# Four pairs in the third pass of w_down, casts of a pair gated by its buffers, two loads in buffers of v, and a longer lag for rows of q and k

## The chip, the cores and the metric

One Trainium2 chip, one of its cores. The metric is the device time of one execution in microseconds (us), the median of the runs. A core has engines that work in parallel, each through its own instructions in a fixed order: TensorE (PE, matmuls), VectorE (DVE), ScalarE (ACT), GpSimd (POOL), and SyncE (SP), which here only starts DMA transfers. An instruction that waits holds up everything behind it on its engine. Matmuls add up in PSUM, in eight banks; all else lies in SBUF.

## The reference

One encoder layer, x of 256 rows by 2048, all in float32:

```python
xn = rms_norm(h, norm1_g)
proj = xn @ w_in                      # 2048 x 5120: q, k, v, ga, gg
q, k = rope(rms_norm(q)), rope(rms_norm(k))
att = rms_norm(diff_attention(q, k, v, lam), subln_g) * (1 - lambda_init)
u = silu(layer_norm(causal_depthwise_conv(ga * sigmoid(gg))))   # 31 taps
h = h + concat([att, u]) @ w_out      # 2048 x 2048
hn = rms_norm(h, norm2_g)
a, bu = hn @ w_gate, hn @ w_up        # 2048 x 5632 each
y = h + (silu(a) * bu) @ w_down       # 5632 x 2048
```

## The kernel before

**Matmuls.** Every operand is split into a rounded part and a residue (`hi` and `lo`), and a product is three matmuls: hi by hi, lo by hi, hi by lo. The weights come as *chunks*, in the order in which they are multiplied. A plain chunk is 128 x 1024 values: SyncE loads it into a `raw` buffer (four of them, `RAW_BUFS`), ScalarE casts `whi` (L342), VectorE subtracts to get `wlo` (L351). For some, marked `by_dma`, ScalarE writes the negated raw into `wlo` (L345) and GpSimd starts a transfer that adds the weights to it (L346). There are four `whi` and four `wlo` buffers.

**Pairs.** In the feed-forward part (FFN) a block of the output is 256 x 1024, from two weight sides of 512 columns: 512 of w_gate and of w_up, or two neighbouring 512s of w_down. Most k-tiles (128 rows of the weights) go in by twos, one unit for each side: 12 matmuls, `multiply_two` (L1112, L1117). Written "g"/"u", or "G"/"U" where the `lo` is made by DMA. Others go in as a *pair* "s": two k-tiles and both sides in seven products by a fast scheme (as Strassen's), 21 matmuls in `multiply_pair` (L1090, L1091, L1092) for the 24 of a g and a u. A pair's weights must be prepared: SyncE loads `wb` (1 MB, L1051, two buffers), VectorE makes sums of them in `wt` (L1057 to L1059, one buffer), ScalarE casts three of its seven parts from `wb` (L1064) and four from `wt` (L1068) into `wh`, VectorE makes the residues `wl` of the three (L1072) and of the four (L1073). `wh` and `wl` have two buffers each. The other operand of a pair has forms of its own too, made by `pair_forms` (VectorE L971 to L976 and L980, ScalarE L965 to L968 and L978).

**The FFN.** Eleven blocks j of w_gate and w_up (j = 0 without pairs), and in three passes (`FGROUPS` = 4, 4 and 3 blocks j) the rows of w_down that those blocks feed; a pass has two blocks of output. `DOWN` has for each pass the k-tiles (j, t) that are pairs, and the order of units in its two blocks. At the end of a block the eight banks are added up: ScalarE copies the first product (L1095), VectorE adds five (`bank_sums`, L1194 to L1199, the first four of which free the banks that the next block's products take), then the g/u units' banks (L1213 in a block of w_gate and w_up, with the multiplication L1215 behind it; L1247 in one of w_down). After a block of w_gate and w_up its activation is transposed by TensorE (L918) into `ps_a` and copied by ScalarE: for a pair by `pair_forms`, else by L953, and for the very last block j = 10 through a copy `ac` (L951) first; VectorE makes its residue (L955).

**The order.** The program is written unit by unit in `run_chunks`; the engines then run in that order. Ahead of unit t's matmuls, a lookahead issues the preparation of later units: residues (`part`), casts from `wb` (`raw`), sums, casts with `lo` by DMA (`dma`), casts (`round`), loads. Each list goes on in order of units, up to some units ahead, and stops at the first that it may not issue. Chains of work beside it (`transposed`, attention) are generators, resumed a step at a time between units; if a unit's operand isn't written yet when its turn comes, they are resumed until it is. `LAG[0]` is the number of such steps by which the rows of q and k (normalisation and rotation, VectorE L704 to L707) are put off. In the same stretch VectorE also does the taps of the convolution (L592).

Of the kernel before, what the change touches and what calls it, by code (L numbers as in the profile page):

```python
# [13 lines left out]
F32 = mybir.dt.float32  # L14
# [5 lines left out]
P = 128  # L20
D = 2048
S = 256
NM = S // P
# [9 lines left out]
N = 512  # L33
# [16 lines left out]
NK = 2  # L50
# [11 lines left out]
RAW_BUFS = 4  # L62
# [1 line left out]

MINUS_FROM = 8

LAG = (3, 2, 6)
HL_BUFS = 4

KTILE_US = 1.30  # L70
# [19 lines left out]

DOWN = (dict(pairs=((1, 0), (1, 1), (2, 0)), order=("sgGsgGgsuUuUu",) * 2),
        dict(pairs=((4, 0), (4, 1), (5, 0)), order=("sgGsgGgsuUuUu",) * 2),
        dict(pairs=((8, 0), (8, 1), (9, 0)), order=("sGsGgsUUu", "sGsGGsUUu")))

RAW_AHEAD = 5
LOAD_AHEAD, DMA_AHEAD, SUMS_AHEAD, HI_AHEAD, LO_AHEAD = 9, 5, 5, 4, 3
# [18 lines left out]
def tile_block(  # L115
# [13 lines left out]
    pre = prestack.enter_context(tc.tile_pool(name="pre", bufs=2))  # L129
# [124 lines left out]
    def resume():  # L254
        for g in list(running):
            if next(g, StopIteration) is StopIteration:
                running.remove(g)
# [36 lines left out]
    chunks = []  # L294
    before = {}

    def block(w, cols, ks, xs, done=None, bkey=None, first=True, last=True, spare=False, cuts=()):

        ks = list(ks)
        cols = [(cols, N)] if isinstance(cols, int) else cols  # L300
        width = sum(n for _, n in cols)
        bkey = bkey if bkey is not None else ("b", len(chunks))
        i = 0
        cuts = list(cuts)
        while i < len(ks):
# [10 lines left out]
    def weights(parts):  # L316

        n = sum(w for _, _, _, w in parts)
        src = wts[next_weight[0] : next_weight[0] + P * n].rearrange("(p n) -> p n", n=n)
        placed_at.append((next_weight[0], n, parts))  # L320
        next_weight[0] += P * n
        return src

    def load_chunk(c):
        view = lambda t: t.rearrange("p (k n) -> p k n", n=c["width"])[:, : c["nk"]]
        c["view"] = view
        if c.get("spare_raw"):
            c["raw"] = view(early.tile([P, 4 * N], F32, tag="wb", name="raw")[:, : NK * N])
        else:
            c["raw"] = view(wp.tile([P, NK * N], F32, tag="raw", name="raw", bufs=RAW_BUFS))  # L330
        ks = c["ks"] if "ks" in c else range(c["k0"], c["k0"] + c["nk"])
        c["src"] = src = weights([(c["w"], k, col, n) for k in ks for col, n in c["cols"]])
        sp.dma_start(out=c["raw"].rearrange("p k n -> p (k n)"), in_=src)
# [75 lines left out]
    loaded, rounded, parted = [0], set(), set()  # L409
    pair_at, two_at = [], []  # L410

    def earlier(at, i, n):

        k = bisect.bisect_left(at, i) - n
        return at[k] if k >= 0 else None
# [38 lines left out]
    def may_round_raw(t, i):  # L454
        c = chunks[i]
        if "sides" not in c:
            return True
        o = earlier(pair_at, i, 2)
        return loaded[0] > i and o is not None and o < t
# [8 lines left out]
    def part_of(i):  # L468
        if i not in parted:
            parted.add(i)  # L470
            round_of(i)
            chunks[i]["split"](chunks[i])

    def run_chunks():
        n = len(chunks)
        pair_at.extend(i for i, c in enumerate(chunks) if "sides" in c)
        two_at.extend(i for i, c in enumerate(chunks) if "kind" in c and "sides" not in c)
        at = dict(part=0, dma=0, sums=0, round=0, minus=0, raw=0)
        first = next(i for i, c in enumerate(chunks) if "kind" in c)

        def until(what, do, stop, only=lambda c: True, may=lambda i: True):
            while at[what] < min(n, stop) and may(at[what]):
                if only(chunks[at[what]]):
                    do(at[what])
                at[what] += 1

        for t in range(n):
            if t >= first - AHEAD:
                until("part", part_of, t + 1 + LO_AHEAD)
                until("raw", lambda i: round_raw(chunks[i]), t + 1 + RAW_AHEAD, lambda c: "sides" in c,  # L490
                      lambda i: i <= t or may_round_raw(t, i))
                until("sums", sums_of, t + 1 + (SUMS_AHEAD if t >= first else 0), may=may_sum)
                until("dma", round_of, t + 1 + DMA_AHEAD, lambda c: c["by_dma"])
                until("round", round_of, t + 1 + (HI_AHEAD if t >= first else LO_AHEAD))
                load_until(t + 1 + LOAD_AHEAD)
            else:
                if t < len(XPARTS):
                    until("part", part_of, t + 2)
                else:
                    until("part", part_of, t + 1 + AHEAD)  # L500
                    until("minus", minus_of, min(t + 1 + MINUS_AHEAD, first), lambda c: c.get("minus"))
                    until("round", round_of, min(t + 1 + ROUND_AHEAD, first))
            part_of(t)
            chunks[t]["multiply"](chunks[t])
            if chunks[t].get("prompt") and chunks[t]["done"]:
                resume()
        while running:
            resume()
# [175 lines left out]
    def qk_rows(key, b, m, ps):  # L684
# [8 lines left out]
        pool.tensor_scalar(f, f, rstd1[m], 0.0, ALU.mult, ALU.add)  # L693
        yield from lag(LAG[0])
        qn = pre.tile([P, G, DH], F32, tag="va", name="qn")
        for j in range(G):
            act.activation(qn[:, j, :], ps[:, j * DH : (j + 1) * DH], AF.Copy, scale=f[:, j : j + 1])
        yield from lag(LAG[1])
        t1 = pre.tile([P, G, DH], F32, tag="vb", name="t1")
# [7 lines left out]
        dve.tensor_tensor(t1, t1, t2, ALU.add)  # L707
        yield from lag(LAG[2])
        yield from room(1)
# [351 lines left out]
    def round_raw(c):  # L1061
        if "hi" not in c:
            c["hi"] = ffn["pool"].tile([P, 7, N], F32R, tag="wh", name="wh", bufs=2)
            act.copy(c["hi"][:, 4:], c["b"][:, 1:])  # L1064
# [206 lines left out]
    for ks, first, last in ((range(0, 4), True, False), (range(4, 6), False, False), (range(6, 8), False, False),  # L1271
                            (range(8, 16), False, True)):
        for n in range(3):
            block("w_out", n * N, ks, fm, (lambda ps, n=n: out_done(n, ps)) if last else None,
                  bkey=("o", n), first=first, last=last, spare=n == 2)
    block("w_out", 3 * N, range(16), fm, lambda ps: out_done(3, ps))
    for i, c in enumerate(chunks[len(XPARTS) : -12]):
        c["spare_raw"] = i % 3 == 2
        c["minus"] = i >= MINUS_FROM and i % 6 == 4
# [59 lines left out]
```

## Time and profile before

| | |
|---|---|
| median of 3 runs | 1037.3 us (1037.26 to 1037.98) |
| the profiled execution | 1037.66 us, its span 1035.9 us |
| TensorE busy | 1028.0 us, 99% of the span |
| VectorE, ScalarE, GpSimd busy | 83%, 66%, 15% |
| memory read and written | 248.80 MB and 8.39 MB |
| granted TensorE clock, mean | 1.00 |

The span is the time from the first to the last instruction of the profiled execution; times inside the trace count from its start. A row of a timeline has start, duration, engine, line, operation, output and inputs, and in brackets the idle time before it and what ended it, where that is long enough to be named. Durations of TensorE overlap: the start of the next instruction tells its pace.

### The profile page before, as it was taken

The numbers are of one execution on the slowest core, as the hardware profiler recorded it, in microseconds if no ns is written. First come the engines' busy times: TensorE is split into PE (matmuls) and PEld (weight loads), VectorE is DVE, ScalarE is ACT, GpSimd is POOL, SyncE is SP. The second block draws the span as 40 slices with busy tenths as digits, with TensorE's granted clock in tenths as the row PEclk, the third lists the DMA queues.
The fourth block names the chain that finished last, engine by engine and source line by source line (L and its number), as shares of the span: only waits on it lengthen the run. The fifth ranks groups of instructions, "written<-read, shape, count | busy, mean of one in ns | idle before, by whom it ended". The sixth has DMA issues, their size and how long they took to land.

```text
span 1035.9 us, 13050 instructions
## 1 busy us (share of the span) xinstructions
PE 1028.0 (99%) x4641; PEld 849.0 (82%) x4641; DVE 862.7 (83%) x1087; ACT 685.8 (66%) x865; POOL 155.1 (15%) x198
## 2 busy tenths in 40 slices
PE   9999999999999999999999999999999999999998
PEld 7888888888888888788888888888888888888886
DVE  6699889897646699999978779999896697998983
ACT  6855567767756577777566667776765666767761
POOL 0040232411100101011011111110101121111121
PEclk9999999999999999999999999999999999999999
DMA  9967775676566669798889998987969999889896
GB/s 341 326 201 239 236 208 187 189 218 183 154 211 224 229 238 262 247 319 240 254 255 292 260 308 263 307 237 241 309 186 286 290 283 327 234 250 299 238 263 130
DMA packets 66065, 258.05 MB, mean 249 GB/s; under 512 B 7376, under 2 KB 8912, under 8 KB 58576
## 3 DMA queue, kind: packets, MB, share of 16 engines
q1 hardware_dynamic: 48944, 201.34, 53.7%
q0 software_dynamic: 16768, 55.58, 28.2%
q8 instruction: 36, 0.59, 0.2%
q10 hardware_dynamic: 288, 0.29, 0.1%
q14 instruction: 29, 0.24, 0.1%
HBM read 248.80 MB, written 8.39 MB: 248 GB/s over the span
## 4 chain that ended last, share of the span: by engine, by line
PE 83%; DVE 9%; DMA 3%; POOL 2%; ACT 1%; issue 1%; DVEq 0%; ACTq 0%
PE q L1112 23%; PE q L1117 12%; PE q L1090 9%; PE q L1091 9%; PE q L1092 9%; PE acc L387 6%; PE acc L381 6%; PE acc L382 6%; DVE y L592 5%; DVE wlo L351 3%; DMA raw<-in_wts_dram 3%; PE ps_a L918 1%; POOL rsq L220 1%; PE ps_s L727 1%; PE ps_o L805 1%
## 5 line engine op out<-in xcount | busy, mean ns | idle before, releaser
L342 ACT CAST whi<-raw 128x1024 fp32r<-128x1024 f32 (+1 forms) x262 | 270.5, 1042 | 102.8 <-PE acc L382 44.4
L351 DVE TENSOR_TENSOR wlo<-raw,whi 128x1024 fp32r<-128x1024 f32 (+1 forms) x174 | 209.1, 1210 | 71.4 <-ACT whi L342 68.4
L381 PE MATMUL acc<-whi,lhi 128*128 128x512 f32 x416 | 164.2, 395 | 1.2 <-ACT whi L342 1.2
L382 PE MATMUL acc<-whi,llo 128*128 128x512 f32 x416 | 162.2, 390 | 0.0
L1073 DVE TENSOR_TENSOR wl<-wt,wh 128x2048 fp32r<-128x2048 f32 x58 | 132.7, 2287 | 20.2 <-ACT wh L1068 20.1
L1064 ACT CAST wh<-wb 128x1536 fp32r<-128x1536 f32 x58 | 86.0, 1484 | 86.9 <-PE q L1091 54.0
L346 POOL DMA_DIRECT2D wlo<-in_wts_dram x74 | 65.1, 891 | 509.7 <-ACT wlo L345 486.0
L1068 ACT CAST wh<-wt 128x2048 fp32r<-128x2048 f32 x58 | 110.5, 1904 | 18.5 <-DVE wt L1059 18.4
L1090 PE MATMUL q<-wh,fhi 128*128 128x512 f32 x280 | 109.1, 390 | 0.4 <-DVE sum L1197 0.4
L1092 PE MATMUL q<-wl,fhi 128*128 128x512 f32 x280 | 109.0, 389 | 0.0
L1091 PE MATMUL q<-wh,flo 128*128 128x512 f32 x280 | 108.9, 389 | 0.0
L1072 DVE TENSOR_TENSOR wl<-wb,wh 128x1536 fp32r<-128x1536 f32 x58 | 101.6, 1751 | 2.1 <-ACT wh L1064 2.1
L592 DVE SCALAR_TENSOR_TENSOR y<-upad,cw,y 128x256 f32<-128x256 f32 x240 | 100.5, 481 | 3.2 <-ACT y L585 3.2
L387 PE MATMUL acc<-wlo,lhi 128*128 128x512 f32 x368 | 100.7, 395 | 0.5 <-DVE wlo L351 0.5
L381 PEld LDWEIGHTS acc<-whi,lhi 128*128 128x128 f32 x416 | 78.1, 188 | 18.4 <-ACT whi L342 2.3
L382 PEld LDWEIGHTS acc<-whi,llo 128*128 128x128 f32 x416 | 78.2, 188 | 16.0
L1117 PE MATMUL q<-wlo,chi 128*128 128x512 f32 x320 | 86.9, 393 | 0.0
L1112 PE MATMUL q<-whi,chi 128*128 128x512 f32 x320 | 85.8, 390 | 0.0
L1112 PE MATMUL q<-whi,clo 128*128 128x512 f32 x320 | 85.6, 389 | 0.0
L387 PEld LDWEIGHTS acc<-wlo,lhi 128*128 128x128 f32 x368 | 68.4, 188 | 14.6 <-DVE wlo L351 0.9
L345 ACT ACTIVATE wlo<-raw 128x1024 fp32r<-128x1024 f32 x74 | 78.2, 1056 | 0.0
L1057 DVE TENSOR_TENSOR wt<-wb 128x1024 f32<-128x1024 f32 x58 | 70.8, 1220 | 2.0 <-DMA wb<-in_wts_dram 1.6
(224 smaller groups left out, 1682.0 us busy)
## 6 DMA issues: line engine op xcount, KB each, us to landing
raw<-in_wts_dram SPq DMA_DIRECT2D x258, 512.0 KB, 5.6
wb<-in_wts_dram SPq DMA_DIRECT2D x57, 1024.0 KB, 7.9
wlo<-in_wts_dram POOLq DMA_DIRECT2D x74, 512.0 KB, 9.3
lod<-in_wts_dram POOLq DMA_DIRECT2D x14, 512.0 KB, 6.4
out_dram<-sum POOLq DMA_DIRECT2D x22, 256.0 KB, 7.2
h<-in_x_dram SPq DMA_DIRECT2D x4, 512.0 KB, 9.1
out_dram<-h POOLq DMA_DIRECT2D x8, 256.0 KB, 3.7
xt<-in_xt_dram SPq DMA_DIRECT2D x6, 256.0 KB, 6.8
```

The source lines that it names most:

```text
L342: act.copy(c["hi"], c["raw"])
L351: dve.tensor_tensor(c["lo"], c["raw"], c["hi"].bitcast(F32), ALU.subtract)
L381: pe.matmul(ps[m], xhi[:, ms], hi[:, j, :], start=c["first"] and j == 0, stop=False)
L382: pe.matmul(ps[m], xlo[:, ms], hi[:, j, :], start=False, stop=False)
L387: pe.matmul(ps[m], xhi[:, ms], lo[:, j, :], start=False, stop=c["last"] and j == nk - 1)
L592: dve.scalar_tensor_tensor(y[:, ct, :], src, wk, y[:, ct, :], ALU.mult, ALU.add)
L1073: dve.tensor_tensor(c["lo"][:, :4], c["t"], c["hi"][:, :4].bitcast(F32), ALU.subtract)
L1090: pe.matmul(ps, fhi[:, f, p, :], c["hi"][:, w], start=bool(first), stop=False)
L1091: pe.matmul(ps, flo[:, f, p, :], c["hi"][:, w], start=False, stop=False)
L1092: pe.matmul(ps, fhi[:, f, p, :], c["lo"][:, w], start=False, stop=bool(last))
L1112: pe.matmul(ps, plain[i][e][:, ms], hi[:, i, :], stop=False, start=i == e == 0 and bool(c["first"].get(qs[m])))
L1117: pe.matmul(sum_bank(c, qs[m]), plain[i][0][:, ms], lo[:, i, :], start=False, stop=i == 1 and bool(c["last"].get(qs[m])))
```

## The change

Lines of the kernel after are 2 to 9 further down than those of before: L351 is then L353, L951 L958, L953 L960, L1064 L1071, L1068 L1075, L1057 to L1059 L1064 to L1066, L1072 and L1073 L1079 and L1080, L1213 L1220, L1215 L1222.

```diff
-LAG = (3, 2, 6)
+LAG = (5, 2, 6)
...
-        dict(pairs=((8, 0), (8, 1), (9, 0)), order=("sGsGgsUUu", "sGsGGsUUu")))
+        dict(pairs=((8, 0), (8, 1), (9, 0), (10, 0)), order=("sGsgsUsu", "sGsgssUu")))
...
         if c.get("spare_raw"):
             c["raw"] = view(early.tile([P, 4 * N], F32, tag="wb", name="raw")[:, : NK * N])
+        elif "raw_tag" in c:
+            c["raw"] = view(pre.tile([P, NK * N], F32, tag=c["raw_tag"], name="raw", bufs=1))
...
         for t in range(n):
             if t >= first - AHEAD:
-                until("part", part_of, t + 1 + LO_AHEAD)
-                until("raw", lambda i: round_raw(chunks[i]), t + 1 + RAW_AHEAD, lambda c: "sides" in c,
+                until("part", part_of, t + 1 + LO_AHEAD, plain)
+                until("pair_part", part_of, t + 1 + LO_AHEAD, pair,
+                      lambda i: i <= t or plain(chunks[i]) or i in rounded)
+                until("raw", lambda i: round_raw(chunks[i]), t + 1 + RAW_AHEAD, pair,
                       lambda i: i <= t or may_round_raw(t, i))
                 until("sums", sums_of, t + 1 + (SUMS_AHEAD if t >= first else 0), may=may_sum)
                 until("dma", round_of, t + 1 + DMA_AHEAD, lambda c: c["by_dma"])
-                until("round", round_of, t + 1 + (HI_AHEAD if t >= first else LO_AHEAD))
+                ahead = HI_AHEAD if t >= first else LO_AHEAD
+                until("round", round_of, t + 1 + ahead, plain)
+                until("pair_round", round_of, t + 1 + ahead, pair, lambda i: i <= t or may_round_raw(t, i))
                 load_until(t + 1 + LOAD_AHEAD)
...
+    for m in range(NM):
+        chunks[RAW_BUFS + m]["raw_tag"] = f"v{m}"
```

In the third pass (10, 0) becomes a fourth pair: 6 matmuls fewer in two blocks. The casts and residues of a pair leave the common lists: a pair's casts are issued ahead of its turn only once it is loaded and the pair two back has been multiplied (`may_round_raw`), its residues only once it is cast. Chunks 4 and 5 (the first of full width) load into the buffers that v takes later, not into `raw` buffers that chunks 0 and 1 used: the wait of their loads for VectorE's L351 is gone, and each of the others that follow uses a `raw` buffer that came free earlier.

Outside of these first loads and of the rows of q and k, the order of instructions differs in two places: the first block with pairs (j = 1) and the end, from the last block j = 10 on. First j = 1, ScalarE's row before (`wh_3687` is the first pair's, `wh_3817` the second's; a name's number differs between the two kernels):

```order
L342 CAST whi_3753<-raw_3727 128x1024 [waits DMAHW0_49,DVE_49,PE_49]
L345 ACTIVATE wlo_3755<-raw_3727 128x1024 [waits PE_49]
L1068 CAST wh_3687<-wt_3600 128x2048
L907 CAST lhi_90<-ps_a_3773 128x512 [waits PE_49]
L907 CAST lhi_90<-ps_a_3778 128x512 [waits PE_49]
L342 CAST whi_3812<-raw_3731 128x1024 [waits DMAHW2_49,DVE_49,PE_49]
L345 ACTIVATE wlo_3814<-raw_3731 128x1024 [waits PE_49]
L1064 CAST wh_3817<-wb_3729 128x1536 [waits DMAHW1_49,DVE_49]
L1068 CAST wh_3817<-wt_3788 128x2048 [waits DVE_49]
```

and after:

```order
L344 CAST whi_3753<-raw_3727 128x1024 [waits DMAHW0_49,DVE_49,PE_49]
L347 ACTIVATE wlo_3755<-raw_3727 128x1024 [waits PE_49]
L914 CAST lhi_90<-ps_a_3772 128x512 [waits PE_49]
L914 CAST lhi_90<-ps_a_3777 128x512 [waits PE_49]
L344 CAST whi_3800<-raw_3731 128x1024 [waits DMAHW2_49,DVE_49,PE_49]
L347 ACTIVATE wlo_3802<-raw_3731 128x1024 [waits PE_49]
L1075 CAST wh_3687<-wt_3600 128x2048
L344 CAST whi_3841<-raw_3839 128x1024 [waits DMAHW4_49,DVE_49,PE_49]
L347 ACTIVATE wlo_3843<-raw_3839 128x1024 [waits PE_49]
L1071 CAST wh_3883<-wb_3729 128x1536 [waits DMAHW1_49]
L1075 CAST wh_3883<-wt_3833 128x2048 [waits DVE_49]
```

The first pair's L1068 has moved behind the next two casts. Two units later L342 and L345 of `raw_3897`, which is loaded behind the fourth pair's `wb`, stand ahead of the third pair's L1068 (of `wh_3889`).

The end, ScalarE before (`ac_8354` and `ac_8398` are the two halves of block 10's activation, `wh_8415` the first pair of the last block):

```order
L345 ACTIVATE wlo_8335<-raw_8214 128x1024 [waits DMASW4_49]
L1068 CAST wh_8331<-wt_8293 128x2048 [waits DVE_49]
L951 COPY ac_8354<-ps_a_8349 128x512 [waits PE_49,Activation_49]
L953 CAST lhi_90<-ac_8354 128x512 [waits Activation_49]
L342 CAST whi_8364<-raw_8247 128x1024 [waits DMAHW6_49]
L345 ACTIVATE wlo_8366<-raw_8247 128x1024 [waits DMASW0_49,PE_49]
L951 COPY ac_8398<-ps_a_8393 128x512 [waits PE_49]
L953 CAST lhi_90<-ac_8398 128x512 [waits Activation_49]
L1064 CAST wh_8415<-wb_8299 128x1536 [waits DMAHW0_49]
```

and after (`wh_8327` is pair (9,0) of the third pass's first block, `wh_8391` pair (10,0), `ac_8402` the half (10,1), which the g that comes next on TensorE reads as `ahi_3466`):

```order
L1071 CAST wh_8327<-wb_8210 128x1536 [waits DMAHW3_49,PE_49,Activation_49]
L1075 CAST wh_8327<-wt_8266 128x2048 [waits DVE_49]
L972 COPY af_8343<-ps_a_8338 128x512 [waits DVE_49,PE_49]
L974 CAST lhi_90<-af_8343 128x2x128 [waits Activation_49]
L975 ACTIVATE lhi_90<-af_8343 128x128
L985 CAST lhi_90<-fs_8368 128x4x128 [waits DVE_49]
L1071 CAST wh_8391<-wb_8272 128x1536 [waits DMAHW5_49,PE_49]
L344 CAST whi_8393<-raw_8274 128x1024 [waits DMAHW6_49]
L1075 CAST wh_8391<-wt_8354 128x2048
L958 COPY ac_8402<-ps_a_8397 128x512 [waits DVE_49,PE_49]
L960 CAST ahi_3466<-ac_8402 128x512 [waits Activation_49]
```

The casts of pair (10,0) now stand ahead of the copy and cast of (10,1). VectorE before, from the residues of pair (8,1):

```order
L1072 TENSOR_TENSOR wl_8272<-wb_8137,wh_8239 128x1536 [waits PE_49,Activation_49]
L1073 TENSOR_TENSOR wl_8272<-wt_8208,wh_8239 128x2048 [waits Activation_49]
L1213 TENSOR_TENSOR sum1_8257<-q6_7994,sum1_8257 128x512 [waits DVE_49,PE_49]
L1213 TENSOR_TENSOR sum3_8259<-q7_8173,sum3_8259 128x512 [waits PE_49]
L1215 TENSOR_TENSOR sum1_8257<-sum1_8257,sum0_8219 128x512 [waits DVE_49,Activation_49]
L1215 TENSOR_TENSOR sum3_8259<-sum3_8259,sum2_8258 128x512 [waits DVE_49,Activation_49]
L1057 TENSOR_TENSOR wt_8293<-wb_8212 128x1024 [waits DMAHW4_49]
L1058 TENSOR_TENSOR wt_8293<-wb_8212,wt_8293 128x512 [waits DVE_49]
L1059 TENSOR_TENSOR wt_8293<-wt_8293,wb_8212 128x512 [waits DVE_49]
```

and after:

```order
L1079 TENSOR_TENSOR wl_8263<-wb_8137,wh_8237 128x1536 [waits PE_49,Activation_49]
L1080 TENSOR_TENSOR wl_8263<-wt_8206,wh_8237 128x2048 [waits Activation_49]
L1064 TENSOR_TENSOR wt_8266<-wb_8210 128x1024 [waits DMAHW3_49,DVE_49]
L1065 TENSOR_TENSOR wt_8266<-wb_8210,wt_8266 128x512 [waits DVE_49]
L1066 TENSOR_TENSOR wt_8266<-wt_8266,wb_8210 128x512 [waits DVE_49]
L1220 TENSOR_TENSOR sum1_8248<-q6_7994,sum1_8248 128x512 [waits PE_49]
L1220 TENSOR_TENSOR sum3_8250<-q7_8171,sum3_8250 128x512 [waits PE_49]
L1222 TENSOR_TENSOR sum1_8248<-sum1_8248,sum0_8217 128x512 [waits DVE_49,Activation_49]
L1222 TENSOR_TENSOR sum3_8250<-sum3_8250,sum2_8249 128x512 [waits DVE_49,Activation_49]
L353 TENSOR_TENSOR wlo_8292<-raw_8139,whi_8270 128x1024 [waits DMASW6_49,DMASW3_49,DMAHW2_49,DMASW0_49,Activation_49]
L1079 TENSOR_TENSOR wl_8351<-wb_8210,wh_8327 128x1536 [waits PE_49,Activation_49]
L1080 TENSOR_TENSOR wl_8351<-wt_8266,wh_8327 128x2048 [waits Activation_49]
```

The sums of the next pair have moved ahead of L1213 and L1215, and the sums of (10,0) come two residues later. In all TensorE has 6 matmuls fewer, VectorE 17 instructions more, ScalarE 3, GpSimd 5 and SyncE 2 fewer.

More of the change, by code (lines that the diff above doesn't have):

```diff
@@ L477, in run_chunks @@
         two_at.extend(i for i, c in enumerate(chunks) if "kind" in c and "sides" not in c)
-        at = dict(part=0, dma=0, sums=0, round=0, minus=0, raw=0)
+        at = dict(part=0, dma=0, sums=0, round=0, minus=0, raw=0, pair_part=0, pair_round=0)
+        plain, pair = (lambda c: "sides" not in c), (lambda c: "sides" in c)
         first = next(i for i, c in enumerate(chunks) if "kind" in c)
```

## The prediction, made before the changed kernel was run

> **What bounds the kernel now.** I read the page first, then the waits of TensorE (columns: who waits on whom, us in total, times, longest).
>
> ```profile
> PE 1028.0 (99%) x4641; PEld 849.0 (82%) x4641; DVE 862.7 (83%) x1087; ACT 685.8 (66%) x865; POOL 155.1 (15%) x198
> ```
>
> ```profile
> PE acc L381 <- ACT whi L342: 1.2, 2, 0.8
> PE acc L387 <- DVE wlo L351: 0.5, 1, 0.5
> PE q L1090 <- DVE sum L1197: 0.4, 1, 0.4
> PE q L1112 <- DVE llo L955: 0.2, 1, 0.2
> ```
>
> TensorE is busy for 99% of the span, and past its first start these four lines are all its waits: 2.3 us. So there is little to win except by fewer matmuls, and whatever makes TensorE wait is paid in full. The other engines are at 66 to 83% on average, but not where the change lies. The two stretches of the third pass's last three blocks (columns: busy us and instructions of each engine, granted clock, DMA share, GB/s):
>
> ```profile
> 962.00:1005.00 43.00, 42.82 (x193) 34.87 (x192) 39.93 (x42) 30.52 (x29) 7.19 (x9) 1.00 0.93 268
> 1005.00:1036.00 31.00, 26.65 (x118) 21.75 (x116) 14.42 (x19) 8.74 (x8) 5.98 (x7) 0.99 0.67 138
> ```
>
> VectorE has 39.93 busy us in 43: cover for TensorE, with 3 us to spare, just where the change gives it more to do.
>
> **Six matmuls fewer.** Pair (10,0) in two blocks stands for a g and a u each time: 21 matmuls for 24. Next, rows of TensorE there (start, duration):
>
> ```profile
> 972.80 0.48 PE L1090 MATMUL q<-wh,lhi 128*128 128x512 f32 x1
> 976.77 0.40 PE L1090 MATMUL q<-wh,lhi 128*128 128x512 f32 x1
> 981.54 0.60 PE L918 MATMUL ps_a<-ident,sum 128*128 128x128 f32 x4
> 981.90 1.18 PE L1112 MATMUL q<-whi,lhi 128*128 128x512 f32 x4
> ```
>
> A pair runs from 976.77 to 981.54, 0.227 us for each of 21; six save 1.36 us. VectorE pays for it: a pair is three sums and two residues.
>
> ```profile
> 969.84 2.28 DVE L1073 TENSOR_TENSOR wl<-wt,wh 128x2048 fp32r<-128x2048 f32 x1
> 972.05 1.28 DVE L1213 TENSOR_TENSOR sum<-q,sum 128x512 f32<-128x512 f32 x2
> 973.25 1.28 DVE L1215 TENSOR_TENSOR sum<-sum,sum 128x512 f32<-128x512 f32 x2
> 974.45 1.22 DVE L1057 TENSOR_TENSOR wt<-wb 128x1024 f32<-128x1024 f32 x1
> 977.04 1.22 DVE L351 TENSOR_TENSOR wlo<-raw,whi 128x1024 fp32r<-128x1024 f32 x1
> 978.17 1.75 DVE L1072 TENSOR_TENSOR wl<-wb,wh 128x1536 fp32r<-128x1536 f32 x1
> 979.84 2.29 DVE L1073 TENSOR_TENSOR wl<-wt,wh 128x2048 fp32r<-128x2048 f32 x1
> ```
>
> From start to start: sums L1057 to L1059 2.59, L351 1.13, L1072 1.67, L1073 2.2; a pair 6.5 us of VectorE for 4.8 of TensorE. Of the queues, SyncE loads a pair's megabyte at once where it loaded two halves, and GpSimd has five accumulating transfers fewer, 15% busy as it is: I cost both at nothing, except where a load waits behind another, below. ScalarE's steps come from its rows, a little further on.
>
> **Third pass, first block.** Times are on the clock of before. (1) VectorE now makes the sums of pair (9,0) ahead of L1213 and L1215. L1213 frees the accumulator that s(8,0)'s last product needs; TensorE took it at 972.80 as L1213 ended its first half. It starts 2.59 later, so TensorE does too: +2.6. (2) VectorE follows on without a hole: L1213/L1215 to 977.0, L351 978.2, residues to 979.9 and 982.15 (2.2 behind L1068, which waits for pair (8,0)'s buffer), the sums of (10,0) to 984.7, then L971 to L974.
>
> ```profile
> 439.84 0.28 DVE L971 SCALAR_TENSOR_TENSOR fs<-af 128x128 f32<-128x128 f32 x1
> 440.77 0.42 DVE L975 TENSOR_TENSOR llo<-af,lhi 128x256 fp32r<-128x256 f32 x1
> 443.68 0.60 ACT L978 CAST lhi<-fs 128x512 fp32r<-128x512 f32 x1
> 982.18 0.59 ACT L951 COPY ac<-ps_a 128x512 f32<-128x512 f32 x1
> 982.79 0.62 ACT L953 CAST lhi<-ac 128x512 fp32r<-128x512 f32 x1
> 983.32 1.48 ACT L1064 CAST wh<-wb 128x1536 fp32r<-128x1536 f32 x1
> 984.70 1.04 ACT L342 CAST whi<-raw 128x1024 fp32r<-128x1024 f32 x1
> 989.15 1.89 ACT L1068 CAST wh<-wt 128x2048 fp32r<-128x2048 f32 x1
> ```
>
> The four operations take 0.93, to 985.7. ScalarE has L978 behind them and then, in its new order, L1064, L342 and L1068 of pair (10,0) ahead of L951 and L953 of (10,1): 0.55 + 1.4 + 0.95 + 1.8 + 0.6 + 0.6 = 5.9, to 991.65. Before, L951 of (10,1) ran at 982.18, before L1064. TensorE's next work in its own order is g(10,1), which reads what L953 writes: it starts at 991.7 for 981.90, having been ready at 984.5. Even a VectorE that was early would not save this: L1064 writes the buffer of pair (8,1), which TensorE reads until about 984. From there the same steps (without L978) end at 989.4: the wait is between 4.9 and 7.2 us; I take 7.2, since VectorE is late by its own sum. The rest of the block is 78 matmuls, 17.7 us, in which nothing else comes late: the last block starts at 1009.4. Before, it started here:
>
> ```profile
> 1000.89 0.39 PE L1090 MATMUL q<-wh,lhi 128*128 128x512 f32 x1
> ```
>
> So +8.5 at that point.
>
> **Last block.** Four pairs are 26.2 us of VectorE; with two plain residues (2.3) and the block's own additions (nine of 0.6, by L1213's pitch) it has 33.9, against 132 matmuls or 29.9 us of TensorE: VectorE bounds it. On top of that, SyncE issues the wb of the fourth pair, and the raws of the last g and u behind it, only when L1072 of the second has freed a buffer, at about 1015.4: eight additions, a L351 and L1072 behind the first block's last pair, whose first products are there at about 1007.8. The next fence shows such a pair of loads in the first FFN block: issued at 398.2 and 398.6, the raw there at 405.2, 6.6 us. With a second raw behind it I take 7.7: 1023.1. ScalarE casts that raw in two steps ahead of the third pair's L1068 (to 1027.3), and L1073 ends at 1029.5. TensorE wants it after 68 matmuls and a wait of 0.35 at the second pair, at 1025.1: 4.4 late; the fourth pair's residue is 1.9 later still, since its sums, the last L351 and both residues follow on VectorE. From 1029.5 there are 64 matmuls (14.5) and that 1.9: the last one ends at 1045.9. Before it ended 135 matmuls after 1000.89, at 1031.5; what lies behind it (additions, output) stays. The third pass costs **+14.4**, its six matmuls inside. Ends: 12 with a raw 2 us quicker, 17 with one 3 us slower, and 7.8 if the last block kept TensorE's pace (8.5 less three matmuls).
>
> **First FFN block of gate and up, about 385 to 433.** Its pairs are also prepared later now, though nothing else changes.
>
> ```profile
> 405.25 1.06 ACT L342 CAST whi<-raw 128x1024 fp32r<-128x1024 f32 x1 [0.20 <-DMA raw<-in_wts_dram]
> 398.21 0.33 SPq L1051 DMA_DIRECT2D wb<-in_wts_dram  x1
> 398.59 0.42 SPq L333 DMA_DIRECT2D raw<-in_wts_dram  x1
> 411.64 0.39 PE L1092 MATMUL q<-wl,fhi 128*128 128x512 f32 x1
> 405.08 2.29 DVE L1073 TENSOR_TENSOR wl<-wt,wh 128x2048 fp32r<-128x2048 f32 x1 [0.31 <-ACT wh L1068]
> 425.86 0.68 DVE L1194 TENSOR_TENSOR sum<-q,sum 128x512 f32<-128x512 f32 x1
> 428.79 0.51 PE L1090 MATMUL q<-wh,fhi 128*128 128x512 f32 x1 [0.42 <-DVE sum L1197]
> ```
>
> L1068 of the first pair now stands behind two more casts (ending about 393.5 for 390.3), so the second pair's L1072 and with it SyncE's wb and the raw behind it go out at about 400 for 398.2, and the raw lands at about 407 for 405.2. ScalarE now casts that raw (L342, L345) ahead of the third pair's L1068, which ends at about 410.6; L1073 follows to 412.9, where TensorE wants it at 411.64. From there VectorE has the fourth and fifth pair, one L351 and the next sums, 17.1 us, ahead of L1194: 430.0 for 425.86. TensorE, which waits for L1197 already, goes on at 433.05 for 428.79: **+4.3** (3.6 to 4.8; 0 if the raw were there at once).
>
> **Start.** Chunks 4 and 5 load into buffers of v.
>
> ```profile
> 6.15 0.33 SPq L333 DMA_DIRECT2D raw<-in_wts_dram  x1
> 10.93 1.05 ACT L342 CAST whi<-raw 128x1024 fp32r<-128x1024 f32 x1 [1.93 <-DMA raw<-in_wts_dram]
> 12.03 0.50 PE L381 MATMUL acc<-whi,lhi 128*128 128x512 f32 x1 [0.84 <-ACT whi L342]
> ```
>
> The load at 6.15 waited for VectorE; it can go at 4.8, so TensorE's hole before 12.03 (0.84, some 1.1 with the slow restart) closes: −1.1. Ends: 0, if the DMA engines only share their rate differently, and −1.4.
>
> **Rows of q and k, two steps later.** VectorE stops for one of them just before TensorE's wait for L351:
>
> ```profile
> 154.16 0.69 DVE L704 TENSOR_TENSOR t<-qn,gcsq 128x512 f32<-128x512 f32 x1 [2.76 <-ACT qn L697]
> ```
>
> With six taps and a residue ahead of it, that wait (0.5, about 0.7 with the restart) goes: −0.7; some such small holes later in attention are worth −0.4 (0.4 either way).
>
> **Sum.** The profiled run took 1037.66 (span 1035.9), 0.36 over the median 1037.3. 1037.66 − 1.1 − 0.7 − 0.4 + 4.3 + 14.4 = 1054.2; on the median 1053.8. I say 1054.
>
> **A rule that would add.** Last, rows that group an instruction (min, median, max ns):
>
> ```profile
> L149 PE MATMUL ps_warm<-ident x17: 287/421/476, 1.4 to 4.8; 128*128 128x128 f32 x17
> L918 PE MATMUL ps_a<-ident,sum x80: 270/272/273, 433.5 to 981.9; 128*128 128x128 f32 x80
> ```
>
> The same transposes take 421 ns at the kernel's start and 272 in its middle: after idling TensorE is slower, for about 4 us, until 5.4. A 7 us wait at g(10,1) could bring that back: 4 us at 272/421 lose 1.4 to 2 us, and the time is 1055 to 1056. The Trainium skill, "TensorE: Matmul & The Clock Gate", Part 1, states that the array's clock halves after an idle window of about 3.4 us and recovers after as long a busy one. The rows bear the slow start out; the granted clock of the stretches quoted reads 0.99 and 1.00, and the trace has no long wait midway to try it on.
>
> **Rivals.** *All waits hidden (faster):* if L951/L953 of (10,1) ended before about 984.5 and VectorE had its 6.5 us per pair over, only the savings are left: 1037.3 − 1.4 − 1.1 − 0.7 − 0.4 = 1033.7. Against it: ScalarE works in order, and L1068 of (10,0) can't run before TensorE leaves (8,1). *The last block keeps up:* 1037.3 − 2.2 + 4.3 + 7.8 = 1047; for it: if wb and raw come early, VectorE can work ahead while TensorE waits at g(10,1). *Only one place costs:* the third pass at its least (+7) or the first block alone, 1039 to 1043.
>
> **How the numbers follow.** Full sum 0.45 and with a slow restart 0.15 (1050 to 1058); last block keeps up 0.2 (1045 to 1049); one place 0.1; all hidden 0.07; within 0.2% (2 us, about what a measurement of this kernel tells from no change) 0.03. Leaving out the hidden cases and half of the one place gives 1041 to 1058. Slower 0.9, same 0.03, faster 0.07.
>
> **What the changed profile would show.** Right: a wait "q <- ACT" of 5 to 7 us at the first g of the third pass's first block, named by the new copy of (10,1); a wait of some 4 us for L1197's counterpart near 429; two waits of TensorE for residues in the last block; the hole at 11 us gone. Wrong: TensorE's busy share back at 99%, or VectorE idle in the last block while TensorE waits for something else, DMA most of all.

## The result, and the profile after

The changed kernel takes 1063.49 us (median of 4, 1062.76 to 1066.06) for 1037.41 of before: 2.5% slower, ratio 1.0254 with a 95% interval of 1.0242 to 1.0266. Forecast were 1054, in a range of 1041 to 1058. The direction was right, and so were the places of the two large losses, the third pass and the first block with pairs; the rows of q and k lost time where a gain was forecast, and the sum was too small by 9.5 us. First, from the page of the kernel after:

```profile
span 1061.9 us, 13021 instructions
PE 1034.8 (97%) x4635; PEld 852.6 (80%) x4635; DVE 879.0 (83%) x1104; ACT 684.2 (64%) x862; POOL 149.5 (14%) x193
PEclk9999999999999999999999999999999999999897
```

TensorE has six matmuls fewer and is busy 6.8 us longer: some of its work ran slower, and the row of granted clock shows a dip at the end. Its longest waits, after:

```profile
PE q L1119 <- ACT ahi L960: 7.0, 1, 7.0
PE q L1097 <- ACT wh L1075: 4.2, 1, 4.2
PE q L1097 <- DVE sum L1201: 2.5, 1, 2.5
PE q L1097 <- DVE sum L1220: 2.5, 1, 2.5
PE q L1099 <- DVE wl L1080: 2.4, 3, 1.1
PE acc L383 <- ACT lhi L835: 1.6, 1, 1.6
```

All but the last stand where the forecast had waits; in the last block it named residues alone, where 4.2 us are a wait for the cast ahead of them. In time (rows of TensorE, start and duration):

```profile
263.74 0.51 PE L383 MATMUL acc<-whi,lhi 128*128 128x512 f32 x1 [1.57 <-ACT lhi L835]
433.25 0.50 PE L1097 MATMUL q<-wh,fhi 128*128 128x512 f32 x1 [2.54 <-DVE sum L1201]
982.13 0.50 PE L1097 MATMUL q<-wh,lhi 128*128 128x512 f32 x1 [2.54 <-DVE sum L1220]
998.48 2.07 PE L1119 MATMUL q<-whi,ahi 128*128 128x512 f32 x4 [6.98 <-ACT ahi L960]
1000.35 1.80 PE L1119 MATMUL q<-whi,alo 128*128 128x512 f32 x4
1037.79 0.79 PE L1097 MATMUL q<-wh,lhi 128*128 128x512 f32 x1 [4.21 <-ACT wh L1075]
1041.13 0.63 PE L1098 MATMUL q<-wh,llo 128*128 128x512 f32 x1
1041.56 0.63 PE L1099 MATMUL q<-wl,lhi 128*128 128x512 f32 x1
1047.89 0.40 PE L1099 MATMUL q<-wl,lhi 128*128 128x512 f32 x1
```

Four matmuls from 998.48 to 1000.35 and from 1041.13 to 1041.56 one: 0.47 and 0.43 us each, twice the usual 0.227. Three stretches of the kernel after (columns as in the prediction, the granted clock third from the end):

```profile
264.62:268.04 3.42, 3.42 (x8) 2.74 (x9) 2.60 (x3) 1.44 (x4) 2.70 (x2) 0.50 0.68 149
998.49:1001.90 3.41, 3.41 (x8) 2.73 (x9) 3.41 (x4) 1.84 (x2) 0.86 (x1) 0.50 0.02 5
1036.04:1046.28 10.24, 7.39 (x17) 5.32 (x18) 8.41 (x7) 5.91 (x4) 0.88 (x1) 0.50 0.31 51
```

The clock is halved for 3.4 us behind two waits and for 8.5 behind the third. Counting how much more than 0.227 us each matmul took there, waits left out, that is 1.7 us behind the first, 1.7 behind the second and 3.3 behind the third. Not all of it is lost: the last of the rows above is the first matmul of the last pair that needs its residue of the four parts, and VectorE writes that residue until 1047.78, 0.1 us earlier (second row below). At the usual pace TensorE would have been there some 3 us sooner, and would have waited. So the first two count in full, 3.4 us, and the third next to nothing.

ScalarE ahead of g(10,1), after:

```profile
992.56 0.62 ACT L985 CAST lhi<-fs 128x512 fp32r<-128x512 f32 x1 [5.20 <-DVE fs L981]
993.09 1.47 ACT L1071 CAST wh<-wb 128x1536 fp32r<-128x1536 f32 x1
994.46 1.04 ACT L344 CAST whi<-raw 128x1024 fp32r<-128x1024 f32 x1
995.40 1.89 ACT L1075 CAST wh<-wt 128x2048 fp32r<-128x2048 f32 x1
997.20 0.57 ACT L958 COPY ac<-ps_a 128x512 f32<-128x512 f32 x1
997.81 0.62 ACT L960 CAST ahi<-ac 128x512 fp32r<-128x512 f32 x1
```

That is the forecast chain, step by step: 5.9 us behind L981's sums. And the last block's loads (SyncE), the casts that wait for them (ScalarE) and the residues of the last two pairs (VectorE):

```profile
1024.02 0.33 SPq L1058 DMA_DIRECT2D wb<-in_wts_dram  x1
1024.39 1.44 SPq L335 DMA_DIRECT2D raw<-in_wts_dram  x2
1033.94 1.04 ACT L344 CAST whi<-raw 128x1024 fp32r<-128x1024 f32 x1 [9.82 <-DMA raw<-in_wts_dram]
1035.85 1.88 ACT L1075 CAST wh<-wt 128x2048 fp32r<-128x2048 f32 x1
1037.77 2.29 DVE L1080 TENSOR_TENSOR wl<-wt,wh 128x2048 fp32r<-128x2048 f32 x1 [7.23 <-ACT wh L1075]
1045.49 2.29 DVE L1080 TENSOR_TENSOR wl<-wt,wh 128x2048 fp32r<-128x2048 f32 x1
```

The raw took 9.5 us, not 7.7, and the third pair's second cast stood behind it. VectorE sat idle for 7.23 us meanwhile: here the load and the order of the casts set the time, not the amount of VectorE's work. That is one of the prediction's own signs of being wrong, though its sum had this wait in it.

By equal matmuls of the two traces, the kernel after is 0.8 us ahead of before at 104 us, 2.4 behind at 286, 6.6 behind from 450 to 960, and 26.0 at the end of the span. So the start gave 0.8, the rows of q and k cost 3.2, the first block with pairs 4.2, and the third pass 19.4. The last block, from its first matmul to its last, took 39.6 us (from 1017.87), where before took 30.4 and the forecast makes 36.3.

### The profile page after: what moved, and what is told of

Same layout as the page of the kernel before. It is cut to its first block, busy times and chain, and to the rows that moved or that the text cites. A ratio compares the mean times of both kernels' runs of the same rounds, so it can differ in the third digit from the quotient of the medians.

```text
span 1061.9 us, 13021 instructions
## 1 busy us (share of the span) xinstructions
PE 1034.8 (97%) x4635; PEld 852.6 (80%) x4635; DVE 879.0 (83%) x1104; ACT 684.2 (64%) x862; POOL 149.5 (14%) x193
## 4 chain that ended last, share of the span: by engine, by line
PE 90%; DVE 4%; ACT 3%; DMA 2%; issue 1%; SPq 0%; DVEq 0%; ACTq 0%
PE q L1119 20%; PE acc L383 11%; PE acc L384 11%; PE acc L389 11%; PE q L1124 10%; PE q L1097 8%; PE q L1099 8%; PE q L1098 8%; DVE wl L1080 2%; DMA raw<-in_wts_dram 1%; ACT wh L1075 1%; PE ps_a L925 1%; DVE wt L1064 1%; ACT whi L344 0%; PE ps_s L734 0%
## 5 line engine op out<-in xcount | busy, mean ns | idle before, releaser
L344 ACT CAST whi<-raw 128x1024 fp32r<-128x1024 f32 (+1 forms) x258 | 266.8, 1041 | 117.0 <-PE acc L384 41.5
L353 DVE TENSOR_TENSOR wlo<-raw,whi 128x1024 fp32r<-128x1024 f32 (+1 forms) x175 | 210.6, 1211 | 76.5 <-ACT whi L344 76.3
L1080 DVE TENSOR_TENSOR wl<-wt,wh 128x2048 fp32r<-128x2048 f32 x60 | 137.3, 2288 | 27.4 <-ACT wh L1075 27.3
L1071 ACT CAST wh<-wb 128x1536 fp32r<-128x1536 f32 x60 | 88.9, 1481 | 88.1 <-PE q L1098 60.6
L348 POOL DMA_DIRECT2D wlo<-in_wts_dram x69 | 60.0, 869 | 527.7 <-ACT wlo L347 486.9
L1075 ACT CAST wh<-wt 128x2048 fp32r<-128x2048 f32 x60 | 114.2, 1903 | 28.7 <-DVE wt L1066 28.7
L1079 DVE TENSOR_TENSOR wl<-wb,wh 128x1536 fp32r<-128x1536 f32 x60 | 105.1, 1752 | 3.9 <-ACT wh L1071 3.9
L1064 DVE TENSOR_TENSOR wt<-wb 128x1024 f32<-128x1024 f32 x60 | 73.3, 1221 | 0.9 <-DMA wb<-in_wts_dram 0.2
L347 ACT ACTIVATE wlo<-raw 128x1024 fp32r<-128x1024 f32 x69 | 72.8, 1055 | 0.0
```

Of the source, the lines that this page charges most:

```text
L344: act.copy(c["hi"], c["raw"])
L353: dve.tensor_tensor(c["lo"], c["raw"], c["hi"].bitcast(F32), ALU.subtract)
L1075: act.copy(c["hi"][:, :4], c["t"])
L1080: dve.tensor_tensor(c["lo"][:, :4], c["t"], c["hi"][:, :4].bitcast(F32), ALU.subtract)
```

## The experiments

The unchanged kernel before ran beside each; its median was 1037.6 to 1037.7 us. Theory A is named in each expectation; the question was whether the parts of the change, each alone, cost what the trace says, and what the half clock follows.

**The lag back at 3** (kernel after).

```diff
-LAG = (5, 2, 6)
+LAG = (3, 2, 6)
```

> The kernel after with LAG[0] back at 3. Theory A (the longer lag makes the attention's last operand late, TensorE waits for it at 263.74 and then runs at half clock for 4 us): the stretch from 125 to 280 us is back to that of before, which is 3.2 us shorter (TensorE was 0.8 us ahead of before at 106 us and 2.4 us behind at 282), so 1060.3 us. Rival B (the moved loads at the start shift transfers and so delay attention): no change, 1063.5 us.

1062.81 us (1060.46 to 1064.04), ratio to before 1.0238 (1.0220 to 1.0255): 0.7 less than after by medians, within the scatter of both, and not the 3.2 of theory A. In the trace the stretch did what theory A says: at the matmul that is 2.4 us behind in the kernel after, this one is 0.8 ahead of before. Most of the gain was lost again later, 2.2 us of it in the first block with pairs, where the clock fell this time and had not before. The first three rows are of the kernel after, the last two of this run (columns as above):

```profile
261.21:264.62 3.41, 1.46 (x7) 0.62 (x5) 0.54 (x2) 3.38 (x8) 0.92 (x1) 1.00 0.69 133
428.46:431.88 3.42, 2.25 (x10) 1.51 (x9) 3.33 (x3) 0.22 (x1) 0.00 (x0) 1.00 0.98 338
431.88:435.29 3.41, 1.76 (x6) 0.97 (x6) 3.18 (x5) 1.91 (x1) 0.00 (x0) 1.00 0.75 305
428.95:432.36 3.41, 1.41 (x6) 0.97 (x6) 3.17 (x5) 1.90 (x1) 0.00 (x0) 1.00 0.98 398
432.36:435.78 3.42, 3.17 (x8) 2.15 (x7) 3.42 (x7) 2.07 (x3) 0.00 (x0) 0.50 0.14 54
```

Where the wait falls decides it. In each of the fourteen traces the granted clock changes only at whole multiples of 3.41 us from one another, a grid that lies elsewhere in each execution; the rows above are steps of it. In the kernel after the 2.54 us wait that ends at 433.25 lies across two steps, which keep 2.25 and 1.76 us of TensorE's work, and the clock stays whole. Here the same wait leaves 1.41 us in one step, and the next one is at half clock. The two short waits at 264 in the kernel after lie in one step, which keeps 1.46 (first row), and the next one is at half clock too. Over the traces, up to their last matmuls, every step at full clock with up to 1.52 us of TensorE's work (30 of them) is followed by one at half clock, and none of the 4180 with 1.58 or more is; at half clock the clock came back behind steps with 2.87 us or more, and not behind those with up to 2.75.

This also fits the scatter: times of one kernel with such waits differ by 1 to 5 us, and where they do, the slower executions mostly show the lower mean clock (of the kernel with g(10,1) two units later, below, two at 1058.9 and 1059.1 us have 0.995 and 0.994, the other two, at 1061.5 and 1062.3 us, 0.990).

**Only the v buffers** (kernel before).

```diff
+        elif "raw_tag" in c:
+            c["raw"] = view(pre.tile([P, NK * N], F32, tag=c["raw_tag"], name="raw", bufs=1))
...
+    for m in range(NM):
+        chunks[RAW_BUFS + m]["raw_tag"] = f"v{m}"
```

> The kernel before with chunks 4 and 5 loaded into buffers of v, nothing else. Theory A: TensorE's wait near 12 us shrinks and the rest keeps its order, as the kernel after shows until 106 us: 0.8 us less, 1036.6 us. Rival B: the loads now share their rate with those of x and land later, or the buffer of v holds up a later load: no gain, 1037.4 us or more.

1036.75 us (10 runs), ratio 0.9992 (0.9982 to 1.0001): the sign is forecast A's, but alone it isn't clear of no change. In its trace, equal matmuls run 0.9 us ahead of before from 200 us to the end. The wait near 12 us didn't close; it is 0.66 for 0.84 us. Of the 0.9 us, 0.55 are there by 104 us, and the rest comes at the wait for L351 near 163 us, which is no longer among the waits listed.

**Only the gate of the pairs' casts** (kernel before, `run_chunks` of after).

> The kernel before with the pairs' casts and residues gated as in the change, still three pairs in the third pass. Theory A: only the first block with pairs is prepared later, TensorE waits there some 4.2 us more, and the end is untouched: 1041.6 us. Rival B (the loss in that block is a shift of transfers that comes from the earlier stretches, not from the order): 1037.4 us.

1042.34 us (1041.80 to 1044.40), ratio 1.0048 (1.0033 to 1.0063). Theory A, for which 1041.6 was forecast. Its longest wait in that block:

```profile
430.90 0.50 PE L1095 MATMUL q<-wh,fhi 128*128 128x512 f32 x1 [2.54 <-DVE sum L1199]
```

**Only the four pairs** (kernel before).

```diff
-        dict(pairs=((8, 0), (8, 1), (9, 0)), order=("sGsGgsUUu", "sGsGGsUUu")))
+        dict(pairs=((8, 0), (8, 1), (9, 0), (10, 0)), order=("sGsgsUsu", "sGsgssUu")))
```

> The kernel before with the third pass's four pairs and unit orders, the lookahead as before. Theory A (the fourth pair itself puts its casts ahead of the copy of (10,1) and makes VectorE the bound of the last block, whatever the gate): most of the 19.4 us that the end lost, 1053 to 1058 us. Rival B (the gate of the casts makes them late): under 1042 us.

1059.27 us (1058.05 to 1060.16), ratio 1.0207 (1.0192 to 1.0222). The fourth pair itself costs the end 21.6 us: theory A, though 1.3 us above the range that it gave. Without the gate g(10,1) waits longer still, and the last block stops at other places:

```profile
994.84 2.08 PE L1112 MATMUL q<-whi,ahi 128*128 128x512 f32 x4 [10.11 <-ACT ahi L953]
1020.37 0.80 PE L1090 MATMUL q<-wh,lhi 128*128 128x512 f32 x1 [4.20 <-DVE sum L1194]
```

**Only the lag of 5** (kernel before).

```diff
-LAG = (3, 2, 6)
+LAG = (5, 2, 6)
```

> The kernel before with LAG[0] = 5, nothing else. Theory A (the longer lag by itself makes attention's last operand late): TensorE waits near 264 us and runs slow behind it, 2 to 3 us lost: 1040 to 1041 us. Rival B (the order after the lag is worth 0.7 as predicted, and the loss at 264 us comes with the other changes at the start): 1037 us or less.

1039.57 us (10 runs), ratio 1.0019 (1.0009 to 1.0029): 1.85 slower, theory A, somewhat less than it said. The waits:

```profile
PE acc L381 <- ACT lhi L828: 1.6, 1, 1.6
PE acc L382 <- DVE llo L830: 0.4, 1, 0.4
```

and, in the two steps of the grid with these waits, the clock stays whole:

```profile
261.72:265.14 3.42, 1.85 (x11) 1.23 (x9) 0.00 (x0) 3.42 (x6) 0.92 (x1) 1.00 0.60 157
265.14:268.55 3.41, 3.03 (x13) 2.25 (x14) 3.15 (x4) 1.93 (x6) 2.21 (x2) 1.00 0.66 132
```

These are the same waits as in the kernel after, here on both sides of a step's end, without the 1.7 us behind them. Three of the ten executions, at 1040.7 to 1040.9 us, have a mean clock of 0.997 or 0.998, the others 0.999 or 1.000. The four parts alone come to -0.95 + 4.6 + 21.6 + 1.85 = 27.1 us, the whole to 26.1.

**TensorE kept busy in two waits** (kernel after; `zeros` is a tile of 128 x 32 zeros that GpSimd fills at the start, `keep_busy` multiplies it).

```diff
-            transpose_two(pt, aa, t)
+            for _ in range(14 if (j, t) == (10, 1) else 1):
+                transpose_two(pt, aa, t)
...
+        if c["sums"] is chunks[-1]["sums"] and p == 2:
+            keep_busy(sum_bank(c, Q6), c["hi"][:, 4], 16)
```

> The kernel after, with work for TensorE that changes no value in two waits: the four transposes of (10,1) are done 14 times instead of once ahead of g(10,1) (5 us of its 7 us wait), and 16 matmuls with zero weights (32 columns) go into an open bank ahead of s(9,0) of the last block. Theory A (TensorE's clock is halved because it idles, so each long wait costs a second time behind it): the granted clock stays at 1.00 behind both, the 8 matmuls at 999 to 1002 and the 19 at 1038 to 1046 that take 0.43 us go back to 0.23, 1.6 and 3.5 us; some 1.9 of the latter come back as the wait for the last pair's residue that the slow clock had covered: 1059 to 1061 us. Rival B (the clock falls for another reason, the load of the chip or the phase of the run): 1063.5 us with slow matmuls as before.

1073.28 us (1071.17 to 1074.42), ratio 1.0341 (1.0325 to 1.0356): neither. Behind both waits the clock was whole, as A says. Behind the second it gained nothing: VectorE takes 7.7 us from the third pair's residue to the last one's, as in the kernel after, and TensorE, now sooner there, waits for it:

```profile
1055.76 0.50 PE L1109 MATMUL q<-wl,lhi 128*128 128x512 f32 x1 [1.25 <-DVE wl L1088]
```

But in the first 240 us a matmul took 0.232 us for 0.227 (medians), at a granted clock of 1.00, and later a little less, and the run was 8.7 us behind the kernel after at 960 us, ahead of the places of the experiment; some 1.2 us of that came at one half-clocked step at 439. New ahead of there are only the small tile and the GpSimd instruction that fills it.

**Only the transposes repeated** (kernel after).

> The kernel after with only the transposes of (10,1) repeated 14 times, nothing added to memory (in the last run with filler the whole program had run 1 to 3% slower between 20 and 980 us, from the first stretches on, where its code was unchanged, and its time can't be compared). Theory A (idling halves the clock): g(10,1) starts about as late as in the kernel after, but its matmuls take 0.23 us, not 0.43: 1.6 us less, 1061 to 1062 us, if VectorE lets TensorE keep it. Rival B: slow matmuls as before, 1063.5 us. The program outside the end runs at the pace of the kernel after in both; if it runs slower again, the small tile was not the reason.

1062.28 us (1060.97 to 1063.45), ratio 1.0231 (1.0215 to 1.0246). Outside of the end it ran at the pace of the kernel after (1.1 us behind it from 536 to 940). The stretch around g(10,1), which began at 1001.0:

```profile
1000.00:1003.00 3.00, 2.05 (x9) 1.70 (x10) 2.07 (x3) 2.77 (x4) 0.00 (x0) 1.00 0.00 0
```

Of the 7.0 us of waiting 1.3 are left, the rest is filled with work, and the clock is 1.00 behind it, where the kernel after had 0.50. So the idling halves the clock, theory A. The time is 1.2 us lower, which the scatter doesn't tell from none; this execution ran at half clock behind the 2.5 us wait at 983 instead.

**g(10,1) two units later** (kernel after).

```diff
-order=("sGsgsUsu", "sGsgssUu")
+order=("sGssUgsu", "sGsgssUu")
```

> The kernel after with the first block of the third pass in the order sGssUgsu: g(10,1) comes two units later, behind s(9,0) and U; ScalarE's order is as it was, so the copy and cast of (10,1) end at about the same time. Theory A (only the place of g in TensorE's order made it wait for casts that stand behind pair (10,0)'s): the 7.0 us wait and the slow clock behind it go, 1055 us. Rival B (VectorE has no time for four pairs in this block either, so s(9,0) or s(10,0) waits for residues instead): 1060 to 1063 us.

1060.29 us (1058.91 to 1062.30), ratio 1.0219 (1.0204 to 1.0235): 3.2 us of the 8.5 that A promised, and the time of B. Two shorter waits of g(10,1) itself stand in the place of the long one:

```profile
1001.95 0.96 PE L1119 MATMUL q<-whi,lhi 128*128 128x512 f32 x3 [1.36 <-ACT ac L958]
1008.10 1.20 PE L1119 MATMUL q<-whi,alo 128*128 128x512 f32 x4 [2.45 <-DVE alo L962]
```

VectorE's residue L962 stands behind the work for two pairs, which VectorE does without a hole from 999.64 on. That fits B's shortage of VectorE, though B had s(9,0) or s(10,0) waiting.

**u for U in the last block** (kernel after).

```diff
-order=("sGsgsUsu", "sGsgssUu")
+order=("sGsgsUsu", "sGsgssuu")
```

> The kernel after with the last block's U as u (order sGsgssuu): its residue is VectorE's (1.1 us more), and ScalarE's cast of the raw that is loaded behind the fourth wb now stands behind the third pair's second cast, not ahead. Theory A (TensorE's 4.4 us wait at s(9,0) and the slow clock behind it come from that cast, which waits for the transfer): 1063.5 less 4.4 and about 2: 1056 to 1058 us. Rival B (VectorE is the bound of this block whatever ScalarE waits for): 1062 to 1065 us.

1059.96 us (1059.31 to 1060.45), ratio 1.0214 (1.0199 to 1.0230): between the two. The wait for the cast at s(9,0) is gone, TensorE waits for residues instead (1.88 us here, 1.24 a little later), and the last block takes 35.6 us for 39.6:

```profile
1040.57 0.50 PE L1099 MATMUL q<-wl,lhi 128*128 128x512 f32 x1 [1.88 <-DVE wl L1079]
```

**Both orders, lag 3** (kernel after).

> The kernel after with both changed orders (sGssUgsu, sGsgssuu) and LAG[0] = 3. If the two waits are independent, the gains add up: 1063.5 - 0.7 - 3.2 - 3.5 = 1056 us. If both orders only move the same shortage of VectorE (its work per block is longer than TensorE's), the second order adds little: 1059 us.

1053.08 us (1051.83 to 1056.85), ratio 1.0151 (1.0134 to 1.0169): 10.4 less than after, 3 us more than the sum of the parts, and below both forecasts. In the last block, which began at 1016.29, there is a single wait of over 0.2 us left,

```profile
1038.52 0.50 PE L1099 MATMUL q<-wl,lhi 128*128 128x512 f32 x1 [1.21 <-DVE wl L1080]
```

and the clock is whole behind it. The block takes 31.2 us, where before took 30.4, although VectorE makes one residue more for it than in the kernel after: here the last block nearly keeps up with TensorE. Why the two orders together give more than their parts isn't shown; four executions from 1051.83 to 1056.85 leave part of it to the clock. The kernel is still 15 us slower than three pairs, nearly all of it lost before the last block.

**First residue on GpSimd** (as the last run, third pass only).

```diff
-        dve.tensor_tensor(c["lo"][:, 4:], c["b"][:, 1:], c["hi"][:, 4:].bitcast(F32), ALU.subtract)
+        third = c["sums"] is chunks[-1]["sums"] or c["sums"] is chunks[-9]["sums"]
+        (pool if third else dve).tensor_tensor(c["lo"][:, 4:], c["b"][:, 1:], c["hi"][:, 4:].bitcast(F32), ALU.subtract)
```

> As the run with both orders, but in the third pass the first residue of each pair (128x1536, 1.75 us on VectorE) is made by GpSimd, which is busy for 14% of the span. Theory A (VectorE's time is what is short there): 8 x 1.7 = 14 us of VectorE gone, TensorE's waits for residues and sums in the last two blocks shrink, 4 to 6 us less than the run with both orders. Rival B (the length of each pair's chain, load to sums to cast to residue, is what is late): no gain, or slower, since the same subtraction takes longer on GpSimd.

1071.87 us (1070.91 to 1074.29), ratio 1.0330 (1.0316 to 1.0344): 18.8 slower than on VectorE, theory B. The line's two groups (ns: least, median, most):

```profile
L1080 DVE TENSOR_TENSOR wl<-wb,wh x52: 1748/1752/1759, 389.3 to 950.3; 128x1536 fp32r<-128x1536 f32 x52
L1080 POOL TENSOR_TENSOR wl<-wb,wh x8: 3475/3772/5221, 962.6 to 1043.0; 128x1536 fp32r<-128x1536 f32 x8
```

GpSimd takes 3.8 us (median) for 1.75. Since the chain to `wb`'s release got longer, this doesn't show that VectorE's time isn't short too.

**A faster kernel: v buffers and a lag of 4** (kernel before).

> The kernel before with the v buffers and LAG[0] = 4, as a candidate for a faster kernel. Theory A (one step more takes away the wait at 163 us and isn't yet late at 265): 1036.75 - 0.7 = 1036 us. Rival B (any later row makes attention late): 1037.5 to 1038.5 us.

1035.63 us (10 runs), ratio 0.9981 (0.9972 to 0.9990): 0.2% less than before, by an interval that doesn't reach 1. TensorE's longest waits, past the first start:

```profile
PE acc L383 <- ACT whi L344: 0.9, 2, 0.7
PE q L1092 <- DVE sum L1199: 0.4, 1, 0.4
```

The wait of before for L351 at 163 us is gone and the one at 264 has not come: theory A. From 160 to 165 us it gains 1.2 us on before, where the v buffers alone gain 0.3.

## Why the prediction was wrong in size

Three steps failed: the half clock, which the sum left out (3.4 us); the rows of q and k, a gain of 1.1 in the sum and a loss of 1.5 even without the half clock; and the last block's chain from load to residue, 3.3 too short.

- **Six matmuls, the third pass.** Right in kind, too small in size. Forecast +14.4, measured 19.4. The waits of 2.6 and 7.2 measured 2.54 and 6.98. The rest is 1.7 us at half clock behind g(10,1), and 3.3 in the last block, whose chain from load to residue was mis-sized. The raw took 9.5 us for the assumed 7.7, so TensorE had the third pair's residue 6.1 us late, not 4.4. The last pair's residue ended 7.7 us behind that one (1040.06 to 1047.78), and the 21 matmuls between take 4.8, so it holds up TensorE by 2.9, whether TensorE waits or runs slowly until then; the 1.9 in the sum doesn't follow from the prediction's own rows, which give 7.6 for the sums, L351 and two residues. Some 0.6 us more in that block aren't placed. (Four pairs at 6.46 us are likewise 25.8, not 26.2.)
- **"VectorE bounds it".** Not borne out for the last block: VectorE sat idle for 7.23 us in it, and with other orders the same four pairs went through in 31.2 us. What was late there were the load and the cast behind it, which the sum did have.
- **First block with pairs.** Right: +4.3 forecast, 4.2 in the trace, 4.6 by the run with the gate alone.
- **Start.** -1.1 forecast, -0.8 in the trace, -0.95 alone. The load went out earlier (at 4.65 us for 6.15), and the wait for it still lasts 0.5 to 0.7 us.
- **Rows of q and k.** This step failed. It counted what the longer lag takes away (the wait for L351, which did go: 1.2 us from 160 to 165) and gave -1.1 with what it called small holes; it didn't ask who waits for those rows in the end. ScalarE, before (first row) and after:

```profile
260.65 0.84 ACT L828 ACTIVATE lhi<-ps_at,cols 128x256 fp32r<-128x256 f32 x2 [0.32 <-PE ps_at L824]
260.87 1.04 ACT L344 CAST whi<-raw 128x1024 fp32r<-128x1024 f32 x1
261.80 1.52 ACT L648 ACTIVATE upad<-upad,lnb,lnr 128x512 f32<-128x512 f32 x2
263.22 0.82 ACT L835 ACTIVATE lhi<-ps_at,cols 128x256 fp32r<-128x256 f32 x2
```

  The last head's transposes came later (260.63 for 260.01), and ScalarE did L835 behind a cast and two steps of the convolution when TensorE already wanted it: 1.6 and 0.4 us of wait. Alone the lag of 5 costs 1.85 us, 3 more than forecast; in the kernel after it costs 3.2, of which 1.7 are half clock.
- **A rule that would add.** This term was left out of the sum: the prediction had the half clock as a rival of 0.15, at one wait, for 1.4 to 2 us. It came at three places. Behind g(10,1) the price was as worked out (1.7), behind the rows of q and k it was 1.7 again, and the 3.3 us in the last block were hidden by the late residue. By the rule of the Trainium skill ("TensorE: Matmul & The Clock Gate", Part 1), an idle window of about 3.4 us halves the clock, and it had to follow from the forecast's own 7 us wait. The trace agrees there: 0.50 behind the 7.0 us wait, and 1.00 where that wait was filled. The Trainium skill says in the same part of that page that the window is free-running and does not start anew with a kernel; the grid of 3.41 us in these traces, which lies elsewhere in each execution, agrees. The traces differ in one thing: the window need not be wholly idle. A step with 1.52 us of work in 3.41 was followed by half clock, so waits of 1.6 and 0.4 us in one step were enough.
- **The sum.** 3.4 at half clock, 3.3 in the last block, 2.6 for the rows of q and k (3.2 less 1.7 at half clock, for -1.1) and 0.3 at the start, less 0.1 in the first block with pairs: 9.5, which is what was missing. The range ended at 1058 because it held one restart at most, and no loss from the lag.
- **Rivals.** "All waits hidden" didn't come, and "the last block keeps up" not in this kernel; with both orders changed it nearly did. In the third pass's first block VectorE's time looks short: there g(10,1), put off, waited for its residue L962. How much of the loss there is VectorE's time, and how much the length of a pair's chain, stays open.

## What to carry to other kernels

Where TensorE is nearly full, price each new wait with the time behind it. By these traces a wait that leaves TensorE less than about 1.5 us of work in a step of 3.41 us is followed by a step at half clock, which costs up to 1.7 us more. A single wait of 1.6 us didn't do it, one of 2.5 us did or didn't with its place on the grid, and two short waits close together count as one. A slow stretch ahead of another wait that doesn't depend on TensorE is hidden by it, so do not add it up twice. Before work is put off, follow it to the last one who reads it, not only to the wait that it was in the way of. And a scheme that saves TensorE's work by giving more to its helpers needs its chains checked block by block, loads and the order of casts as well as busy time: here 1.36 us saved on TensorE cost 19.4 in the third pass.

## What had not been expected of the hardware

- With one more tile of 128 bytes a partition, matmuls ran up to 2.2% slower (0.232 for 0.227 us, medians of the first 240 us) at a granted clock of 1.00; without it, and else the same up to the end, the pace was back. The cause (an address of the operands?) wasn't tried.
- The granted clock is set in steps of 3.41 us: it fell to 0.50 behind each step with up to 1.52 us of TensorE's work, never behind one with 1.58 or more, and came back behind a step with 2.87 or more, on one core alone at work.
- GpSimd took 3.5 to 5.2 us for a subtraction of 128 x 1536 that VectorE does in 1.75.
